# Splitting the attention's keys and queries in the dense stretch, with its sums on one engine

## The chip, the core and the metric

The kernel runs on one core of a Trainium2 chip. TensorE (PE) multiplies matrices into PSUM banks; VectorE (DVE), ScalarE (ACT) and GpSimd (POOL) do the elementwise work; SyncE (SP) issues most of the DMAs. Each engine works through its own queue of instructions in order, and semaphores tie the queues together: an instruction at the head of a queue that waits holds everything behind it. The metric is the device time of one execution in microseconds.

## What is computed

One layer of a hybrid encoder over 2048 tokens (a grid of 32 rows of 64) of width 1024. From the reference, cut:

```python
h = (_layernorm(x) * (1.0 + scale) + shift).astype(x.dtype)
proj = h @ w_in[l]
q_h, i_h, zf_fw, zf_bw, g_h, q_n, k_n, v_n, g_n = jnp.split(proj, split_pts, axis=-1)
y_hg = _hgrn2_branch(q_h, i_h, zf_fw, zf_bw, g_h, ...)
o_na = _neighbourhood_attention(na_heads(q_n), na_heads(k_n), na_heads(v_n), rpb[l])
y_na = o_na * jax.nn.silu(g_n)
y = jnp.concatenate([y_hg, y_na], axis=-1) @ w_out[l]
z = DEEPNORM_ALPHA * x + gate * y
x = _layernorm(z) * ln_g[l] + ln_b[l]
```

The neighbourhood attention has 16 heads of 64 columns; each query looks at a window of 8 rows by 16 columns. All is float32.

## The kernel before

TensorE takes its operands in a reduced form of float32. To keep the precision, every operand is split in a **high part** (a rounded copy, made by ACT) and a **low part** (the rest, a subtraction on DVE), and each product is three matmuls: high·high, high·low, low·high. So every weight, every tile of `h`, every key and query costs one ACT copy and one DVE subtraction before PE can use it.

The program goes through these stages, in one order on PE that is written out in the code:

- **Startup** (0 to about 91 us): LayerNorm and modulation of the first 1024 tokens in 16 blocks, two groups `g` of 512 tokens with 8 column tiles `k` each. Each block transposes x on PE (L236), ACT shifts and scales it (L241) and makes the high part (L243), DVE the low part (L1271), and PE then multiplies it with the first key, query and gate weights (L282). Between blocks, `values` (a generator over `vproj`, L295 on PE, evacuated on ACT at L303) computes the first part of the attention's values.
- **Dense stretch** (`dense_half`, to about 268 us): first `ahead()` gives PE a gate projection and more values, while `sum_piece` (L1405 on) makes the sums of h blocks that a seven-product scheme for 2x2 blocks needs: four additions of high and low on POOL (L1412), four sums on DVE (L1416), and a split of each (ACT L1419, DVE L1420). Then, for head pairs 1 to 7, class `Pair` multiplies the sums with combinations of the weights: `combine` (L1445 to 1450, POOL) and `prepare` (a split at L1459 and L1460) two products ahead, and `product` (L1475 on PE), whose results, keys `nk` and queries `nq` of 1024 tokens, go unsplit to DRAM.
- **First half of the attention** (`first_half`, to about 556 us): eight head pairs with four slots each. `natten_woven` computes scores (L1081, L1086, L1088), adds the bias and takes the maximum (DVE L1097), then exponent (ACT L1102), normalization (L1106, L1107), transposes (PE L1130, copied by DVE L1134 and ACT L1136) and the sum over the values (L1152). Between them `second_stream` gives PE dense work (L282, L295), and the second 1024 tokens of x are read (L199), measured (L206, L207), scaled and turned to h tiles `hs` in DRAM (`piece`: L241, L245, L250 and two stores, L1564 and L1565). What a slot prepares for the next pair stands in `first_next`: fetch keys and queries (`fetch_top`, L986), split them (`q` at L1000 to 1003, `k` at L1016 to 1018), load values (L1027) and bias tables (L757 to 759).
- The **HGRN recurrence** (to about 1740 us), the **second half of the attention** (to about 2270 us, prepared by `prep_next`), the **output projection**.

A key tile takes both heads of a pair, 64 partitions each. The score matmuls want `KA`, head 0's high part in both halves of the partitions, `KB`, the same of head 1, and `KL`, the low parts of both. `k` makes them by a copy on ACT, a DMA from half to half issued by POOL (L1017), and a subtraction on DVE. The first half has two sets of these tiles, so that one pair's can be made while the other's are read. In the second half there is one set, filled in pieces as the rows of the pair before come free.

On ACT, DVE, POOL and SP the order follows a scheduler that simulates the program, with high priorities where the code says so; in the startup SP, ACT and DVE are in code order as well. `pinned` keeps an instruction in code order. A tile takes one of its tag's buffers and waits until that is free: h tiles in flight to DRAM have three (`"s": 3`).

## Time and profile before

| | |
|---|---|
| three runs | 2586.09, 2587.28 (median), 2588.41 us |
| profiled execution | 2583.36 us |
| its span | 2581.4 us |
| busy: PE, DVE, ACT, POOL | 2529.1, 1883.8, 1502.3, 373.4 us |

The profile follows one execution; its span runs from the first instruction to the last. "Busy" is the time in which an engine executed something. For an engine that sets the pace, the idle time matters, and what ended it; for the others, idle time costs nothing by itself. A row `a <- b` names the instruction that waited and the work that released it. The granted clock is the share of its full speed that TensorE was allowed. Numbers behind L are lines of the kernel before.

### The profile page before, as it was taken

The page shows a single profiled execution, that of the slowest core. Times are in us where ns is not written, and L with a number is a line of the kernel's source. Part 1 is how long each engine was busy: PE and PEld are TensorE (multiplying, and loading weights), DVE is VectorE, ACT ScalarE, POOL GpSimd, SP SyncE. Part 2 cuts the span into 40 slices and gives each one's busy share as a digit, 9 for nine tenths or more (in the row PEclk, how much of TensorE's full clock was granted, in tenths as well). Part 3 has the DMA queues.
Part 4 walks back from the last instruction along what each step waited for, and adds up shares of the span by engine and source line. Part 5 has one row for each costly group of instructions (what it writes and reads, how often), then busy time and mean ns, then how long its engine had stood idle before and what let it go on. Part 6 is the DMA issues. An engine that isn't in the chain of part 4 may idle for free.

```text
span 2581.4 us, 46541 instructions
## 1 busy us (share of the span) xinstructions
PE 2529.1 (98%) x17040; PEld 2138.8 (83%) x17040; DVE 1883.8 (73%) x4567; ACT 1502.3 (58%) x2991; POOL 373.4 (14%) x485
## 2 busy tenths in 40 slices
PE   8899998999999999999999999999999999999998
PEld 7788877788888888888888888999888888888887
DVE  7745566668777778878778878746677778867776
ACT  5323355567666666767666666546677777752331
POOL 0422211200000000000000000011122222323542
PEclk9899999999999999999999999999999999999999
DMA  7445766612211115421222223345466667764452
GB/s 293 127 142 144 198 168 184 189 60 70 70 64 64 57 66 177 170 84 50 78 83 82 87 83 89 99 123 163 119 142 144 140 141 164 181 207 135 158 171 97
DMA packets 233604, 326.94 MB, mean 127 GB/s; under 512 B 42791, under 2 KB 115111, under 8 KB 232231
## 3 DMA queue, kind: packets, MB, share of 16 engines
q1 hardware_dynamic: 208383, 275.23, 35.1%
q0 software_dynamic: 24992, 48.73, 8.2%
q8 instruction: 134, 2.20, 0.4%
q14 instruction: 95, 0.78, 0.1%
HBM read 238.49 MB, written 77.08 MB: 122 GB/s over the span
## 4 chain that ended last, share of the span: by engine, by line
PE 80%; DVE 3%; DMA 2%; issue 1%; ACT 1%; POOL 0%; DVEq 0%; POOLq 0%; SPq 0%; ACTq 0%
PE pj L282 45%; PE pj L295 4%; PE ps L1839 3%; PE ps L1837 3%; PE ps L1838 3%; PE ps L1152 3%; PE ps L1130 3%; PE ps L488 2%; PE ps L480 2%; PE ps L1081 1%; PE ps L555 1%; PE ps L1086 1%; PE ps L584 1%; PE ps L586 1%; PE ps L527 1%
## 5 line engine op out<-in xcount | busy, mean ns | idle before, releaser
L282 PE MATMUL pj<-h,wh 128*128 128x512 f32 x3536 | 1130.1, 401 | 1.2 <-ACT vt L303 1.1
L282 PEld LDWEIGHTS pj<-h,wh 128*128 128x128 f32 x3536 | 640.0, 189 | 133.2 <-issue 10.1
L282 PE MATMUL pj<-h,wl 128*128 128x512 f32 x1768 | 695.0, 393 | 0.0
L282 PEld LDWEIGHTS pj<-h,wl 128*128 128x128 f32 x1768 | 333.0, 188 | 73.3
L295 PE MATMUL pj<-wh,h 128*128 128x256 f32 x1024 | 200.7, 289 | 10.8 <-ACT e L797 5.7
L1102 ACT ACTIVATE pbuf<-pbuf,mx 128x480 f32<-128x480 f32 (+5 forms) x256 | 152.4, 597 | 99.0 <-DVE mx L1097 98.4
L1097 DVE CUSTOM_DVE_ANT_1 pbuf<-ps,bias 128x480 f32<-128x480 f32 (+5 forms) x256 | 129.2, 539 | 86.7 <-PE ps L1086 61.1
L295 PEld LDWEIGHTS pj<-wh,h 128*128 128x128 f32 x1024 | 166.9, 195 | 14.8 <-ACT e L797 6.5
L273 DVE TENSOR_TENSOR wl<-wr,wh 128x512 fp32r<-128x512 f32 x192 | 131.4, 685 | 40.2 <-ACT wh L272 38.2
L272 ACT ACTIVATE wh<-wr 128x512 fp32r<-128x512 f32 x192 | 120.2, 626 | 68.5 <-PE pj L282 62.1
L295 PE MATMUL pj<-wl,h 128*128 128x256 f32 x512 | 146.6, 286 | 0.0
L1821 POOL TENSOR_TENSOR yl<-yr,yh 128x512 fp32r<-128x512 f32 (+1 forms) x80 | 108.6, 1367 | 148.6 <-ACT yh L1820 115.6
L1136 ACT ACTIVATE pt<-ps 120x384 f32<-120x384 f32 (+3 forms) x128 | 65.3, 510 | 95.3 <-PE ps L1130 94.8
L1130 PE MATMUL ps<-ident,pbuf 128*128 128x128 f32 (+2 forms) x832 | 114.7, 275 | 1.5 <-ACT s L241 0.6
L1130 PEld LDWEIGHTS ps<-ident,pbuf 128*128 128x128 f32 (+2 forms) x832 | 98.0, 138 | 19.9 <-DVE pbuf L1107 1.9
L474 DVE TENSOR_TENSOR de<-e,de 128x512 f32<-128x512 f32 x64 | 44.3, 691 | 87.8 <-ACT de L473 87.8
L1820 ACT ACTIVATE yh<-yr 128x512 fp32r<-128x512 f32 (+1 forms) x80 | 47.9, 607 | 102.0 <-PE ps L1838 42.2
L1107 DVE TENSOR_SCALAR pbuf<-pbuf,mx 128x480 f32<-128x480 f32 (+5 forms) x256 | 100.5, 414 | 3.0
L295 PEld LDWEIGHTS pj<-wl,h 128*128 128x128 f32 x512 | 100.0, 195 | 1.1
L1134 DVE COPY pt<-ps 120x384 f32<-120x384 f32 (+3 forms) x128 | 74.8, 584 | 34.2 <-PE ps L1130 33.4
L773 POOL MEMSET pbuf<- 128x248 f32 x8 | 2.1, 306 | 655.2 <-DVE pm L573 641.9
L455 DVE TENSOR_TENSOR_SCAN c<-c,g 128x128 f32<-128x128 f32 x256 | 88.6, 406 | 7.4 <-ACT c L445 7.4
(399 smaller groups left out, 5440.2 us busy)
## 6 DMA issues: line engine op xcount, KB each, us to landing
wr<-in_w_in SPq DMA_DIRECT2D x264, 256.0 KB
yr<-yq SPq DMA_DIRECT2D x78, 256.0 KB
bias<-tint POOLq DMA_DIRECT2D x24, 480.0 KB, 7.9
x<-in_x SPq DMA_DIRECT2D x32, 256.0 KB
ada<-in_ada_m SPq DMA_DIRECT2D x8, 1024.0 KB
wr<-in_w_v SPq DMA_DIRECT2D x32, 256.0 KB
nv<-vt SPq DMA_DIRECT2D x32, 256.0 KB
hs<-s SPq DMA_DIRECT2D x32, 256.0 KB
```

The costliest lines, as they stand in the source:

```text
L272: act.activation(hi, raw, AF.Copy)
L273: dve.tensor_tensor(lo, raw, hi, op=ALU.subtract)
L282: pe.matmul(pz, a, b, start=(k == 0 and n == 0), stop=(k == KT - 1 and n == 2))
L295: pe.matmul(pzs[tp][:, i * 256:(i + 1) * 256], a, b, start=(k == 0 and n == 0 and i == 0), stop=(k == KT - 1 and n == 2), skip_group_check ...
L455: dve.tensor_tensor_scan(c[:, sl], c[:, sl], L[:, sl], 0.0, op0=ALU.add, op1=ALU.subtract)
L1097: return dve.tensor_tensor_reduce(s[:, 0:nk].rearrange("p (r c) -> p r c", c=kw), sc[:, 0:nk].rearrange("p (r c) -> p r c", c=kw), bt[:, 0 ...
L1102: act.activation(s[:, 0:nk], s[:, 0:nk], AF.Exp, scale=-1.0, bias=mx[:, 0:1], accum_out=mx[:, 1:2])
L1107: dve.tensor_scalar(s[:, 0:nk], s[:, 0:nk], mx[:, 2:3], 1.0, op0=ALU.mult, op1=ALU.mult)
L1130: pe.transpose(ptp[0:cw, c * P:(c + 1) * P], s[:, c * cw:(c + 1) * cw], ident)
L1152: pe.matmul(self.po[R][hs_, j * P:(j + 1) * P], v[:, hh * 64:hh * 64 + 64], pts[hh][0:n * KW[j], c * P:(c + 1) * P], start=(c == 0), stop= ...
L1821: pool.tensor_tensor(lo[:, c], src[:, c], hi[:, c], op=ALU.subtract)
L1837: pe.matmul(bank, yh[:, kk], wh, start=start, stop=False, skip_group_check=True)
```

## The change

Four things are done at once.

**The sums.** `sum_piece` makes its four additions on DVE, and lets the four sums come before the four splits; `combine` runs on DVE too. POOL has no arithmetic left in the dense stretch. The second chunk of the value projection no longer stands between startup blocks: `startup` returns the generator, and `ahead()` runs it behind the last block. The four `sum_piece` calls come at steps 0, 3, 6, 9 of that longer stream (0, 4, 8, 10 of the shorter one before). While `feed.fast` is set, a weight's split has a high priority and is not pinned.

**The splits.** `product` splits keys (j = 2 and 5) and the queries of the first 512 tokens (j = 6) at once and stores high and low parts, `nkh` and `nqs`. Queries of the other half (j = 4) are stored unsplit, as before.

**The loads.** For pairs 1 to 7 the first half of the attention loads `KA`, `KB`, `KL` and both query tiles ready-made, seven DMAs on SP in slots 0 and 1 of the pair before, with no work on ACT, DVE or POOL. In the second half the pieces `k0` and `k1` of these pairs come the same way by five DMAs each, issued by POOL. Pair 0 stays as it was.

**The pieces of x.** Loads, statistics, rates and scaling of the second 1024 tokens are cut in smaller portions with a slot each (`at`), and the `hs` tiles move from a tag with three buffers to one with four (`"hb": "bk"`).

```diff
-            self.keep = p in (0, 7) if half else p > 0
+            self.keep = half and p in (0, 7)
...
+        def keys_in(self, o, at, dma=dma):
+            keys, n = keysets[self.p % len(keysets)], o.stop - o.start
+            for z, x in (("KA", slice(0, 64)), ("KB", slice(64, 128))):
+                for y in (slice(0, 64), slice(64, 128)):
+                    dma(keys[z][y, o].bitcast(F32), nkh_d[self.p][0, x, at:at + n])
+            dma(keys["KL"][:, o].bitcast(F32), nkh_d[self.p][1, :, at:at + n])
...
+            if self.half and i < 2 and self.p:
+                return self.keys_in(slice(a * GW, b * GW), (KBASE[1] + a) * GW, nc.gpsimd.dma_start)
...
-        return {0: [(st.fetch_top,), (st.v, 0)], 1: [(st.table, "top", 0), (st.v, 1), (st.k, 0)], 2: [(st.v, 2), (st.k, 1), (st.q, 0)],
-                3: [(st.table, "top", 1)]}
+        return {0: [(st.top_keys,), (st.v, 0)], 1: [(st.table, "top", 0), (st.top_queries,), (st.v, 1)], 2: [(st.v, 2)], 3: [(st.table, "top", 1)]}
...
-    NB0 = {"V": 6, "pbuf": 4, "pt": 4, "yv": 1, "bias": 3, "x": 8, "s": 3}
+    NB0 = {"V": 6, "pbuf": 4, "pt": 4, "yv": 1, "bias": 3, "x": 8, "s": 2}
...
-            pool.tensor_tensor(a, block_of(name, k, 0), block_of(name, k, 1), op=ALU.add)
+            dve.tensor_tensor(a, block_of(name, k, 0), block_of(name, k, 1), op=ALU.add)
...
+            if j in (2, 5):
+                hi, lo = tl("kh", F32R), tl("kh", F32R)
+                act.activation(hi, c, AF.Copy)
+                dve.tensor_tensor(lo, c, hi, op=ALU.subtract)
+                g = int(j == 5)
+                for i, z in enumerate((hi, lo)):
+                    dma(nkh_d[self.u][i, :, g * GRP:(g + 1) * GRP], z.bitcast(F32))
+            elif j == 4:
+                dma(nq_d[self.u][:, GRP:2 * GRP], c)
+            elif j == 6:
+                self.st.q(0, c)
+                for i, z in enumerate(self.st.Q.pop(0)):
+                    dma(nqs_d[self.u][i], z.bitcast(F32))
...
+            for _ in values:
+                feed.tick()
+                yield
             yield from gate_stream(preps[1], feed, (1,))
...
-            if i in (0, 4, 8, 10):
-                sum_piece((0, 4, 8, 10).index(i))
-            if i == 8:
+            if i in (0, 3, 6, 9):
+                sum_piece(i // 3)
+            if i == 14:
                 pairs[0].load(0)
...
-            a, b = short(F32R), short(F32R)
+            a, b = tl("hb", F32R), tl("hb", F32R)
...
-        for g, i in ((0, 3), (1, 16)):
-            slots[i].append((rows, g))
-            slots[i + 1].append((stats, g, 0))
-            slots[i + 2].append((stats, g, 2))
-            slots[i + 3].append((scale, g, 0))
-            slots[i + 6].append((scale, g, 1))
+        for g, at in ((0, (0, 1, 2, 3, 3, 4, 5, 6, 7, 8, 9, 11, 12, 10)), (1, (14, 15, 18, 18, 16, 17, 20, 21, 22, 22, 23, 25, 26, 24))):
```

What this does to the queues is shown at three places; lines there are those of each version, so L282 and L295 of before are L284 and L297 of the changed kernel.

PE at the end of the startup, before: the last matmuls of one block (`h_120` and `h_121` are the high and low part of an h tile, `q_421` and `q_422` of a weight), then the values (`pj`), of which twelve rows like these stand between each two blocks of the second group.

```order
L282 MATMUL ps_697<-h_120,q_421 128x512
L282 MATMUL ps_697<-h_121,q_421 128x512
L282 MATMUL ps_697<-h_120,q_422 128x512
L295 MATMUL pj_718<-wh_529,h_120 128x256
L295 MATMUL pj_718<-wl_530,h_120 128x256
L295 MATMUL pj_718<-wh_529,h_121 128x256
```

The same place of the changed kernel, and the end of the last block.

```order
L284 MATMUL ps_697<-h_120,q_421 128x512
L284 MATMUL ps_697<-h_121,q_421 128x512
L284 MATMUL ps_697<-h_120,q_422 128x512
L284 MATMUL ps_695<-h_122,vt_425 128x512
L284 MATMUL ps_695<-h_123,vt_425 128x512
L284 MATMUL ps_695<-h_122,gt_426 128x512
L284 MATMUL ps_696<-h_122,bk_417 128x512
L284 MATMUL ps_696<-h_123,bk_417 128x512
L284 MATMUL ps_696<-h_122,bk_418 128x512
L284 MATMUL ps_697<-h_122,q_421 128x512
L284 MATMUL ps_697<-h_123,q_421 128x512
L284 MATMUL ps_697<-h_122,q_422 128x512
```

The blocks follow each other directly, and all 96 of these value matmuls come behind the last.

DVE around the last low part of h, before: `h_119` to `h_123` are low parts, `wl` a weight's, `q_` the sums and `S_` the sums' low parts; the `sg` tiles come from POOL.

```order
L1271 TENSOR_TENSOR h_119<-sg_843,h_118 128x512
L1271 TENSOR_TENSOR h_121<-sg_873,h_120 128x512
L849 TENSOR_TENSOR wl_899<-wr_632,wh_898 128x512
L1271 TENSOR_TENSOR h_123<-sg_907,h_122 128x512
L1416 TENSOR_TENSOR q_986<-sg_978,sg_980 128x512
L1416 TENSOR_TENSOR q_992<-q_986,sg_982 128x512
L1420 TENSOR_TENSOR S_0_1_189_989<-q_986,S_0_0_188_988 128x512
L1416 TENSOR_TENSOR q_998<-sg_982,sg_978 128x512
```

The same place of the changed kernel; L1423 are the additions that were POOL's, L1286 is L1271 of before, L1427 and L1431 are L1416 and L1420.

```order
L1286 TENSOR_TENSOR h_119<-sg_781,h_118 128x512
L1286 TENSOR_TENSOR h_121<-sg_799,h_120 128x512
L1423 TENSOR_TENSOR sg_864<-h_108,h_109 128x512
L1423 TENSOR_TENSOR sg_866<-h_116,h_117 128x512
L1423 TENSOR_TENSOR sg_868<-h_92,h_93 128x512
L1427 TENSOR_TENSOR q_872<-sg_864,sg_866 128x512
L1286 TENSOR_TENSOR h_123<-sg_817,h_122 128x512
L1423 TENSOR_TENSOR sg_870<-h_100,h_101 128x512
L1427 TENSOR_TENSOR q_874<-q_872,sg_868 128x512
L1423 TENSOR_TENSOR sg_944<-h_110,h_111 128x512
L1431 TENSOR_TENSOR S_0_1_183_889<-q_872,S_0_0_182_888 128x512
```

Four operations of the sums now stand ahead of the last low part of h, and the weight's split has gone from between.

SP in the first half of the attention, before, while pair 2 is prepared: `bk` are unsplit queries and keys, `wr` weights of the dense work, `nv` the values' way to DRAM, `x` the second half of x.

```order
L199 DMA x_3049<-in_x 128x512
L838 DMA wr_2810<-in_w_in 128x512
L986 DMA bk_3104<-nq 128x512
L838 DMA wr_2890<-in_w_in 128x512
L838 DMA wr_2932<-in_w_v 128x512
L986 DMA bk_3106<-nk 128x256
L986 DMA bk_3473<-nk 128x512
L307 DMA nv<-vt_3004 128x2x256
```

The changed kernel, pair 2's keys and queries.

```order
L840 DMA wr_3015<-in_w_in 128x512
L992 DMA KA_549_2596<-nkh 64x768 x2
L992 DMA KB_550_2597<-nkh 64x768
L840 DMA wr_3057<-in_w_v 128x512
L992 DMA KB_550_2597<-nkh 64x768
L993 DMA KL_551_2598<-nkh 128x768
L1001 DMA q_3311<-nqs 128x512
L1001 DMA q_3312<-nqs 128x512
L309 DMA nv<-vt_3121 128x2x256
```

Seven loads replace three; the first write to a tile waits until PE has read what the pair two before left there.

More of the change, by code (lines that the diff above doesn't have):

```diff
@@ L1388, in startup @@
                 next(values)
-            else:
+            elif not g:
                 next(values, None)
-            if g:
-                feed.tick()
-        for _ in values:
-            pass
-        return rows, feed, first
+        return rows, feed, first, values
     AB = {"11": (0, 0), "12": (0, 4), "21": (1, 0), "22": (1, 4)}
@@ L1543, in first_half, with rows, stats, rates @@
         pipe, xs = [], {}
[L1545 to L1559 removed]
+        mvs, how, sts = {}, {}, {}
+        def rows(g, a, rs):
+            if g not in xs:
+                xs[g], mvs[g] = [[None, None] for _ in range(4)], x_mv()
+            for i in rs:
+                xs[g][i][a] = tl("x")
+                r0 = (2 + g) * GRP + i * P
+                dma(xs[g][i][a], x[r0:r0 + P, a * 512:(a + 1) * 512])
+        def stats(g, a, rs):
+            for i in rs:
+                if a == 0:
+                    sts[g, i] = cp.tile([P, 2, 6], F32, tag="bnst", name=nm("bnst"), bufs=4)
+                pinned(dve.bn_stats(sts[g, i][:, a, :], xs[g][i][a]))
+                if a:
+                    dve.bn_aggr(mvs[g][:, i, :], sts[g, i])
+        def rates(g):
+            how[g] = x_rates(mvs[g])
+        def scale(g, a, rs):
+            x_scale(xs[g], how[g], a, rows=rs, pin=pinned)
         def piece(g, k):
[L1562 removed]
+            a, b = tl("hb", F32R), tl("hb", F32R)
             h_piece(xs[g], k, a, b)
@@ L1647, in body @@
         with phase("st", SB_, SMS), tc.manual_schedule(engines={getattr(mybir.EngineType, e) for e in ("PE", "SP", "Activation", "DVE")}):
-            raws, feed, first = startup()
+            raws, feed, first, values = startup()
         with phase("sa", SA_, SMA):
@@ L1651, in body @@
             second = Chunks(second_srcs())
-            dense_half(preps, feed, first, second)
+            dense_half(preps, feed, first, values, second)
         with phase("n0", NB0, SM0):
```

81 lines of the change are left out of this document (40 added, 41 removed).

## The prediction

> **What bounds the kernel now.** I read the table of windows first, cut at the stages: first projections and sums (80 to 140 us), the seven pairs of dense products (140 to 280), the first half of the attention (280 to 560), the recurrence, the second half of the attention. Columns are stretch, length, busy us of PE, PEld, DVE, ACT and POOL, granted clock, DMA share, GB/s.
>
> ```profile
> 80.00:140.00 60.00, 48.82 (x306) 45.24 (x305) 44.03 (x43) 22.99 (x40) 30.68 (x19) 0.89 0.35 115
> 140.00:280.00 140.00, 140.00 (x622) 115.92 (x621) 78.30 (x128) 47.33 (x80) 38.56 (x39) 1.00 0.57 152
> 280.00:560.00 280.00, 261.53 (x1687) 216.65 (x1686) 175.55 (x514) 148.34 (x333) 50.48 (x96) 0.96 0.59 166
> 560.00:1740.00 1180.00, 1179.54 (x8952) 1004.73 (x8951) 910.59 (x2209) 769.99 (x1419) 7.09 (x21) 1.00 0.27 88
> 1740.00:2270.00 530.00, 528.87 (x3742) 448.00 (x3740) 400.71 (x1204) 372.28 (x855) 121.20 (x209) 1.00 0.63 151
> ```
>
> TensorE is the bound nearly everywhere: 140.00 of 140, 1179.54 of 1180, 528.87 of 530 us. The change removes no matmul, so where PE never idles nothing can be won. It idles 60 − 48.82 = 11.2 us in the first stretch and 280 − 261.53 = 18.5 us in the third; those two are what the change can reach. The list of PE's waits says for whom (us in total, times, longest); first 80 to 140, then 280 to 560:
>
> ```profile
> PE pj L295 <- ACT vt L303: 5.1, 1, 5.1
> PE pj L295 <- ACT e L797: 5.0, 1, 5.0
> PE pj L282 <- ACT vt L303: 1.1, 1, 1.1
> ...
> PE ps L1081 <- DVE mx L1097: 5.4, 2, 3.4
> PE ps L236 <- DVE pt L1134: 5.2, 1, 5.2
> PE ps L1081 <- issue: 3.3, 2, 2.0
> PE ps L1081 <- DMA KB<-KB: 1.8, 4, 1.1
> PE ps L1081 <- DVE pbuf L1107: 1.2, 1, 1.2
> PE ps L1130 <- ACT s L241: 0.6, 1, 0.6
> PE pj L295 <- ACT e L797: 0.4, 1, 0.4
> ```
>
> A gap costs more than itself, since the granted clock falls behind it. Three short windows around gaps:
>
> ```profile
> 98.00:108.00 10.00, 4.99 (x24) 4.78 (x24) 10.00 (x10) 3.71 (x7) 6.94 (x5) 0.66 0.23 65
> ...
> 334.00:346.00 12.00, 8.51 (x44) 6.43 (x43) 9.20 (x33) 6.00 (x16) 3.41 (x7) 0.75 0.54 160
> ...
> 312.00:320.00 8.00, 5.83 (x22) 4.52 (x22) 3.30 (x11) 1.50 (x6) 1.84 (x4) 0.79 0.98 237
> ```
>
> The clock's loss is 10 × 0.34 = 3.4 us, 12 × 0.25 = 3.0 and 8 × 0.21 = 1.7. Over the stages it is 60 × 0.11 = 6.6 and 280 × 0.04 = 11.2 us. About 2.6 of the 6.6 falls into time in which PE idled anyway. So the ceiling is 11.2 + 4.0 = 15 us in the first stretch and 18.5 + 11.2 = 30 in the third, 45 together.
>
> **Where a short gap counts.** The 2.00 us gap at 314 stands in the window of 0.79: gaps of 2 us already slow PE. The Trainium skill, "TensorE: Matmul & The Clock Gate", says under "Why this matters for your kernels" that the clock drops for idle gaps over about 3 us; by that the 2 us gaps here cost themselves only, and some 5 us of the third stretch's clock loss would not come back. The row differs, and I go by the row.
>
> **Sums on DVE alone.** Groups of 80 to 126 us (busy, mean ns | idle before), DVE, then POOL, then ACT:
>
> ```profile
> L1420 DVE TENSOR_TENSOR S<-q,S 128x512 fp32r<-128x512 f32 x16 | 18.1, 1155 | 0.0
> L1416 DVE TENSOR_TENSOR q<-sg,sg 128x512 f32<-128x512 f32 x8 | 7.6, 955 | 0.0
> L1416 DVE TENSOR_TENSOR q<-q,sg 128x512 f32<-128x512 f32 x4 | 5.8, 1460 | 0.2
> ...
> L1416 DVE TENSOR_TENSOR q<-sg,q 128x512 f32<-128x512 f32 x4 | 4.9, 1222 | 0.0
> L1271 DVE TENSOR_TENSOR h<-sg,h 128x512 fp32r<-128x512 f32 x2 | 1.4, 692 | 3.8 <-ACT h L243 3.8
> ...
> L1412 POOL TENSOR_TENSOR sg<-h,h 128x512 f32<-128x512 f32 x14 | 23.1, 1671 | 10.9 <-DVE q L1416 5.5 <-DVE h L1271 5.3
> ...
> L1419 ACT ACTIVATE S<-q 128x512 fp32r<-128x512 f32 x16 | 10.0, 629 | 22.4 <-DVE q L1416 22.4
> ```
>
> Thirty-two additions on DVE take 36.4 us, 1.14 each; the same form away from POOL's takes 0.69 (L1271). ACT waits 22.4 us for them, and its evacuations e and vt stand behind those waits in its queue; that is how PE's two 5 us gaps come about. The change moves POOL's 16 additions over: 48 × 0.69 = 33.1 us on DVE in place of 36.4, with POOL silent. So the sums alone get only 3 us shorter. The larger part is order: the weight splits are put ahead of sums (feed.fast), and the second chunk of the value projection moves from between the last startup blocks to just behind them:
>
> ```profile
> 85.58 0.28 PE L295 MATMUL pj<-wh,h 128*128 128x256 f32 x1
> ...
> 87.02 0.63 PE L282 MATMUL ps<-h,vt 128*128 128x512 f32 x2
> ```
>
> Twelve matmuls take 87.02 − 85.58 = 1.44 us in each of eight blocks, 11.5 us of PE work that no longer delays the last h tile and covers the sums instead. Its price: a block has 1.44 us less cover for its own chain, transpose, ACT twice, DVE once. I take 2.3 us lost there, since near the end four sums stand ahead of h's last low part (4 × 0.69 = 2.8 us less what is idle). Behind it I count about 1.0 at the gate stream, 0.7 at its evacuation, 2.2 where two splits of sums stand ahead of vt on ACT (3 × 0.63): 6.2 us lost in place of 15. **Gain 9**, bounds 5 (the 3 us of DVE and part of the order) and 13.
>
> **Splits in the dense products.** Each of seven pairs gains on DVE two low parts, four combines from POOL and two half-width low parts: 8 × 0.69 = 5.5 us; ACT gets four copies by 0.63, 2.5 us; SP three more stores. In the stretch DVE goes from 78.3 to 78.3 + 38.6 = 117 of 140 us, ACT from 47 to 65. Combines and splits of before:
>
> ```profile
> L1450 POOL TENSOR_TENSOR gt<-wr,gt 128x512 f32<-128x512 f32 x3 | 4.8, 1588 | 19.0 <-DVE wl L1460 13.4 <-DMA wr<-in_w_in 5.7
> ...
> L1460 DVE TENSOR_TENSOR wl<-gt,wh 128x512 fp32r<-128x512 f32 x19 | 14.6, 767 | 8.0 <-ACT wh L1459 8.0
> ```
>
> A split of 767 ns against 692 shows that POOL's 28 combines disturbed DVE little here; silence returns about 3 us, which leaves 114 of 140 and PE the bound. Zero. If the cover is gone (eight operations of a pair in a row hold the next weights), a pair loses up to 1.5 us, seven 10.
>
> **First half of the attention.** Per pair 1 to 7 the change drops ACT's copies and DVE's low parts of keys and queries, and POOL's copies from half to half; five key loads and two query loads on SP take their place, a slot or more ahead. Groups of 280 to 560, then what DVE waited for there:
>
> ```profile
> L206 DVE BATCH_NORM_STATS2 bnst<-x 128x6 f32<-128x512 f32 x16 | 10.2, 671 | 0.1
> ...
> L1018 DVE TENSOR_TENSOR KL<-bk,KB 64x512 fp32r<-64x512 f32 (+1 forms) x14 | 7.8, 556 | 0.4
> L1018 DVE TENSOR_TENSOR KL<-bk,KA 64x512 fp32r<-64x512 f32 (+1 forms) x14 | 7.6, 545 | 2.8 <-ACT KA L1016 2.8
> ...
> L1003 DVE TENSOR_TENSOR q<-bk,q 64x512 fp32r<-64x512 f32 x7 | 4.8, 688 | 0.2
> L1002 DVE TENSOR_TENSOR q<-bk,q 64x512 fp32r<-64x512 f32 x7 | 4.8, 685 | 0.4 <-ACT q L1000 0.2
> ...
> DVE s L245 <- DMA hs<-s: 12.5, 2, 8.2
> ```
>
> DVE loses 7.8 + 7.6 + 4.8 + 4.8 = 25 of 175.6 us. By cause:
> - copies KA/KB: "issue" 2.0 (the other 1.3 is pair 0's, which keeps them) and KB 1.8, with 1.7 of clock: 5.5, all gone.
> - mx, 5.4 and about 5.1 of clock: eight of L206, the key splits and the scale chain stand ahead of L1097. The change spreads statistics over four slots and takes the splits out. Three quarters: 7.9.
> - pt, 5.2 and 3.4: L245 held DVE 8.2 us until a store of hs released one of three buffers. Now four, with x's loads spread. Four fifths: 7.
> - the rest, 2.2 and 1.7: half, 2.
>
> That is 22.4. The key loads are new on SP, in order, waiting for PE's scores of two pairs before, with weight loads queued behind. By the rows the cost lies between nothing (a pair has 280 / 8 = 35 us, and they go out a pair ahead) and one 2 us gap with its 1.7 per pair, 7 × 3.7 = 26. I take 2.4, nearer to nothing, as there are several slots. **Gain 20**, bounds 0 and 28.
>
> **Second half.** Keys k0 and k1 of pairs 1 to 7 come by ten loads on POOL in place of four copies on POOL, two fetches on SP and eight instructions on ACT and DVE. POOL's copies, a bias load and its use:
>
> ```profile
> L1017 POOL DMA_DIRECT2D KA<-KA x37 | 19.9, 538 | 72.6 <-ACT KA L1016 59.7 <-PE ps L1086 12.1
> ...
> 1894.66 0.63 POOL L755 DMA_DIRECT2D bias<-tint  x1
> ...
> 1902.24 0.66 DVE L1097 CUSTOM_DVE_ANT_1 pbuf<-ps,bias 128x480 f32<-128x480 f32 x1 [0.39 <-PE ps L1086]
> ...
> DMA to landing us min/median/max: 4.0/6.9/15.1
> ```
>
> Six more issues by 0.54 are 3.2 us per pair, in two places; behind them wait the bias loads, one of which has 1902.24 − 1894.66 = 7.6 us for a landing of 6.9. PE is full here, so nothing can be won. Zero, bounds a gain of 1 (PE's idle) and a loss of 43 (below).
>
> **Sum.** The profiled execution took 2583.36 us: 2581.4 of span and 2.0 around it. 2583.4 − 9 − 20 = 2554.4. The median of the runs shown, 2587.28, is 3.9 above that execution; kept, this gives **2558.3**.
>
> **Rivals.**
> - *Bias late in the second half* (the slower side). If 3.2 us of later issue and 2 of slower landing (a quarter of the way from 6.9 to the longest, 15.1) make a bias 5.2 late, 4.5 past the slack of 0.7, that is 6.2 with 1.7 of clock, in seven pairs 43: 2558 + 43 = 2601. From about 35 us, 5 per pair, the kernel is measurably slower. For it: the short slack above, DMA share 0.63. Against: POOL idled 72.6 us before those copies, and they waited in the same queue. Chance 0.07.
> - *Key loads late in the first half*: SP's queue holds them, the gaps stay under another name, and only the start's 9 and a part return: 2587.3 − 13 = 2574. For it: DMA share 0.98 around 314. Against: a pair's lead. Chance 0.15.
> - *DVE bounds the sums*: 48 additions with splits between them still reach the first product late; the start gives 1: 2566. For it: 33 against 36 us. Chance 0.15.
> - *The change doesn't do what it says*: the spread pieces of x meet new waits and everything cancels: 2587. Chance 0.06.
> - *Clock by the long gaps only*: the 2 us gaps' clock loss stays, 5 us: 2563. The row of 0.79 speaks against. Chance 0.03.
>
> My forecast (gain 20 to 42) has 0.54. Range 2545 (42 of the ceiling of 45) to 2581: it leaves out half the fourth rival, the first, and tails, about 0.17. 0.2% is 5.2 us, about what a measurement of this kernel can tell from no change. Faster: 0.54 + 0.15 + 0.15 + 0.03 = 0.87; same 0.06; slower 0.07.
>
> **What would show it.** Windows of 80 to 140 with POOL near nothing, DVE's sums at about 0.69 and clock over 0.95; the waits on e and vt below 2.5 us. In 280 to 560 PE over 274 busy, no wait for KB, pt or hs. In 1740 to 2270 PE still above 528. Wrong if PE waits for key or query loads, for the ps banks in the products, or for the bias.

## The result and the profile after

| | before | changed |
|---|---|---|
| four runs, median | 2586.69 us (2582.83 to 2588.41) | 2563.34 us (2561.01 to 2564.43) |
| ratio, 95% interval | | 0.9911 [0.9893, 0.9928] |
| profiled execution | 2583.36 us | 2563.62 us |
| its span | 2581.4 us | 2561.8 us |

The change saves 0.9%. It was forecast at 2558.3 us, in a range of 2545 to 2581. In two of the experiments below, one execution of four was far longer than the others (8833.1 and 4168.6 us), and the medians given there leave it out. Where the 19.5 us of span went is seen best from PE's own marks, read from the timelines of both kernels (us of each stage; a stage ends with the first matmul of the next, and the second half of the attention is counted from its first score with low parts):

| stage on PE | before | changed | difference | forecast |
|---|---|---|---|---|
| to the first dense product | 134.66 | 123.45 | −11.2 | −9 |
| the 49 dense products, first to last | 133.08 | 133.08 | 0 | 0 |
| last product to the first score ("the join") | 18.58 | 24.71 | +6.1 | none made |
| first score to the recurrence | 260.25 | 242.69 | −17.6 | −20 |
| recurrence | 1201.40 | 1201.21 | −0.2 | 0 |
| second half of the attention | 556.62 | 560.14 | +3.5 | 0 |
| output projection | 276.80 | 276.56 | −0.2 | 0 |

The windows of the changed kernel, with the same columns as before (stretch, length, busy of PE, PEld, DVE, ACT, POOL, granted clock, DMA share, GB/s):

```profile
80.00:140.00 60.00, 59.13 (x393) 54.27 (x392) 43.86 (x71) 25.06 (x44) 0.00 (x0) 1.00 0.39 125
140.00:280.00 140.00, 136.17 (x602) 112.75 (x601) 99.90 (x169) 60.42 (x102) 7.81 (x17) 0.98 0.62 187
280.00:560.00 280.00, 269.29 (x1858) 224.96 (x1858) 172.56 (x528) 144.56 (x328) 33.23 (x66) 0.99 0.71 187
...
1740.00:2270.00 530.00, 525.80 (x3656) 441.46 (x3655) 388.02 (x1171) 356.68 (x821) 141.71 (x247) 1.00 0.64 157
```

The first row is full: PE 59.13 of 60 us at a clock of 1.00, from 48.82 at 0.89. The third has 269.29 in place of 261.53. The second and the last have each lost some 3 to 4 us of PE. PE's list of waits (us in total, times, longest) says where, first 60 to 130 us, then 250 to 560, then 1700 to 2270. Line numbers are now those of the changed kernel (and in an experiment's rows, those of that run's kernel, which can lie a few lines further on):

```profile
PE ps L284 <- DVE h L1286: 0.7, 2, 0.5
PE pj L297 <- ACT vt L305: 0.5, 1, 0.5
PE pj L297 <- ACT e L799: 0.3, 1, 0.3
...
PE ps L238 <- ACT pt L1152: 7.2, 1, 7.2
PE ps L1097 <- DVE mx L1113: 1.5, 1, 1.5
PE pj L297 <- ACT wh L851: 1.4, 1, 1.4
...
PE ps L1097 <- DMA KA<-KA: 2.1, 1, 2.1
PE ps L1097 <- DMA yr<-yq: 1.1, 2, 0.5
```

The two 5 us waits of the start (e, vt) are 0.3 and 0.5. In the first half of the attention the maximum (mx) went from 5.4 to 1.5 and no wait for KA or KB is left, but the wait of a transpose for a bank (L238, in the kernel before L236) has grown from 5.2 to 7.2. It is now the largest single wait of the kernel between the startup and the end.

### The profile page after: what moved, and what is told of

It is laid out like the page before. It is cut to its first block, busy times and chain, and to the rows that moved or that the text cites. A ratio compares the mean times of both kernels' runs of the same rounds, so it can differ in the third digit from the quotient of the medians.

```text
span 2561.8 us, 46445 instructions
## 1 busy us (share of the span) xinstructions
PE 2519.8 (98%) x17040; PEld 2130.8 (83%) x17040; DVE 1869.9 (73%) x4569; ACT 1483.0 (58%) x2949; POOL 316.1 (12%) x455
## 4 chain that ended last, share of the span: by engine, by line
PE 88%; DVE 2%; DMA 2%; issue 1%; ACT 1%; POOL 0%; SPq 0%; DVEq 0%; POOLq 0%; ACTq 0%
PE pj L284 46%; PE pj L297 6%; PE ps L1486 5%; PE ps L1874 3%; PE ps L1873 3%; PE ps L1872 3%; PE ps L1168 3%; PE ps L1146 3%; PE ps L490 2%; PE ps L482 2%; PE ps L1097 2%; PE ps L557 1%; PE ps L1102 1%; PE ps L586 1%; PE ps L588 1%
## 5 line engine op out<-in xcount | busy, mean ns | idle before, releaser
L284 PE MATMUL pj<-h,wh 128*128 128x512 f32 x3536 | 1127.2, 400 | 0.0
L284 PEld LDWEIGHTS pj<-h,wh 128*128 128x128 f32 x3536 | 638.5, 188 | 131.5 <-issue 10.1
L284 PE MATMUL pj<-h,wl 128*128 128x512 f32 x1768 | 693.6, 392 | 0.9 <-DVE wl L854 0.9
L284 PEld LDWEIGHTS pj<-h,wl 128*128 128x128 f32 x1768 | 331.9, 188 | 74.2 <-DVE wl L854 1.3
L1118 ACT ACTIVATE pbuf<-pbuf,mx 128x480 f32<-128x480 f32 (+5 forms) x256 | 152.4, 597 | 125.1 <-DVE mx L1113 124.5
L1113 DVE CUSTOM_DVE_ANT_1 pbuf<-ps,bias 128x480 f32<-128x480 f32 (+5 forms) x256 | 129.2, 540 | 113.3 <-PE ps L1102 73.9
L297 PE MATMUL pj<-wh,h 128*128 128x256 f32 x1024 | 198.4, 288 | 4.9 <-ACT vt L305 1.8
L297 PEld LDWEIGHTS pj<-wh,h 128*128 128x128 f32 x1024 | 165.1, 194 | 9.2 <-ACT vt L305 2.6
L297 PE MATMUL pj<-wl,h 128*128 128x256 f32 x512 | 146.0, 285 | 0.4 <-DVE wl L854 0.4
L1152 ACT ACTIVATE pt<-ps 120x384 f32<-120x384 f32 (+3 forms) x128 | 65.1, 509 | 94.1 <-PE ps L1146 93.5
L297 PEld LDWEIGHTS pj<-wl,h 128*128 128x128 f32 x512 | 99.2, 194 | 1.4 <-DVE wl L854 0.6
```

Source lines behind the costliest of these rows:

```text
L284: pe.matmul(pz, a, b, start=(k == 0 and n == 0), stop=(k == KT - 1 and n == 2))
L297: pe.matmul(pzs[tp][:, i * 256:(i + 1) * 256], a, b, start=(k == 0 and n == 0 and i == 0), stop=(k == KT - 1 and n == 2), skip_group_check ...
L1113: return dve.tensor_tensor_reduce(s[:, 0:nk].rearrange("p (r c) -> p r c", c=kw), sc[:, 0:nk].rearrange("p (r c) -> p r c", c=kw), bt[:, 0 ...
L1118: act.activation(s[:, 0:nk], s[:, 0:nk], AF.Exp, scale=-1.0, bias=mx[:, 0:1], accum_out=mx[:, 1:2])
```

## Experiments: the start

Each edit is against the changed kernel ("−" is the changed kernel). Times are medians; ratios are against the kernel before on the same chip. Stage times come from one profiled execution of each kernel, and kernels whose edit doesn't touch a stage still differ there: the first dense product came at 122.4 to 123.8 us in eight kernels, the first half of the attention took 242.0 to 245.1 us in five, and the second half 557.3 to 562.0 us in twelve. Differences below these widths aren't read.

**The additions back on POOL**, everything else as changed.

```diff
-            dve.tensor_tensor(a, block_of(name, k, 0), block_of(name, k, 1), op=ALU.add)
+            pool.tensor_tensor(a, block_of(name, k, 0), block_of(name, k, 1), op=ALU.add)
```

> The changed kernel with the sixteen additions of high and low parts back on POOL (the combines of the weights stay on DVE). Two theories of the start's gain, read at the first product's matmul (134.7 us from the span's start before, 123.5 changed). Order theory: the gain comes from the value matmuls behind the last block and from splits that go ahead of sums; POOL's additions slow DVE's to about 1.1 us again, but most of the cover stays: first product at 126 to 129, the whole 3 to 5 us slower than the changed kernel. Port theory: the gain comes from POOL being silent; then nearly all is lost: first product at 132 or later, the whole 8 to 12 us slower.

Measured 2574.02 us, ratio 0.9949 [0.9931, 0.9966]; the first product at 134.96 us. The whole 11 us of the start are gone, though the new order is in place. The groups of this run, 78 to 126 us on DVE, then POOL's to 128 us (count, busy, mean ns, idle before):

```profile
L1431 DVE TENSOR_TENSOR S<-q,S 128x512 fp32r<-128x512 f32 x16 | 14.8, 951 | 0.0
L854 DVE TENSOR_TENSOR wl<-wr,wh 128x512 fp32r<-128x512 f32 x6 | 7.3, 1220 | 0.0
...
L1423 POOL TENSOR_TENSOR sg<-h,h 128x512 f32<-128x512 f32 x13 | 21.8, 1701 | 8.6 <-DVE q L1427 7.4 <-DVE h L1286 1.2
```

and the changed kernel's, 78 to 122 us:

```profile
L1431 DVE TENSOR_TENSOR S<-q,S 128x512 fp32r<-128x512 f32 x16 | 10.9, 689 | 2.1 <-ACT S L1430 2.1
L1423 DVE TENSOR_TENSOR sg<-h,h 128x512 f32<-128x512 f32 x14 | 9.4, 688 | 0.0
...
L854 DVE TENSOR_TENSOR wl<-wr,wh 128x512 fp32r<-128x512 f32 x6 | 4.1, 690 | 0.0
```

Weight splits, too, take 1.22 us each in place of 0.69 while POOL adds, six of them 3.2 us more. DVE's idle time before its rows is 0.0 with POOL adding: it didn't stand waiting for POOL's results, it was slow. PE again waits for vt (4.15 us at 96) and e (5.72 us at 111), as in the kernel before.

**The order of before, the sums on DVE.** The value matmuls stand between the startup blocks again, `feed.fast` is never set, the sums come at steps 0, 4, 8, 10.

```diff
-            elif not g:
+            else:
                 next(values, None)
+            if g:
+                feed.tick()
+        for _ in values:
+            pass
...
-            feed.fast = True
             preps[1].raws["g"][0] = first
-            for _ in values:
-                feed.tick()
-                yield
...
-            if i in (0, 3, 6, 9):
-                sum_piece(i // 3)
-            if i == 14:
+            if i in (0, 4, 8, 10):
+                sum_piece((0, 4, 8, 10).index(i))
+            if i == 8:
```

> The changed kernel with the order of the start undone: value matmuls again between the startup blocks, sums again at steps 0, 4, 8, 10, splits of weights pinned and without priority; the sums stay on DVE alone. Order theory: first product at 129 to 133 us, the whole 6 to 10 us slower than the changed kernel. Port theory: with POOL silent the sums are fast wherever they stand: first product at 124 to 126, the whole within 3 us of the changed kernel.

Measured 2561.18 us, 0.9904 [0.9887, 0.992]; the first product at 120.29 us, 3.2 us earlier than in the changed kernel. So the new order costs about 3 us at this mark, where the prediction had most of the 9 us from it; the whole time is the same within its interval. The window of 60 to 80 us of the changed kernel, then of this one:

```profile
60.00:80.00 20.00, 19.24 (x95) 14.96 (x94) 11.19 (x22) 11.97 (x18) 0.00 (x0) 1.00 0.56 148
```

```profile
60.00:80.00 20.00, 20.00 (x129) 18.04 (x127) 8.04 (x17) 9.41 (x15) 0.00 (x0) 1.00 0.57 143
```

PE loses 0.76 us there, since part of a block's chain is no longer covered. Behind it the changed kernel's waits on vt and e, 0.5 and 0.3, are gone here as well: from 15 to 258 us this run has no gap of PE of over 0.2 us. Together that is 1.6 of the 3.2 us; the rest wasn't resolved. The four sums ahead of the four splits and the combines on DVE stay as changed in this run.

Both experiments can be read from ACT's wait for the sums, behind which e and vt stand in its queue. It was 22.4 us in the kernel before. Here it is from 60 to 126 us with the additions back on POOL, in the changed kernel, and with the order of before:

```profile
ACT S L1430 <- DVE q L1427: 19.7, 11, 3.5
```

```profile
ACT S L1430 <- DVE q L1427: 7.1, 6, 3.6
```

```profile
ACT S L1434 <- DVE q L1431: 6.3, 2, 6.0
```

It follows the engine of the additions and not the order.

**The additions on DVE, and the same sixteen again on POOL** into tiles that nobody reads, so that both engines are busy and nothing depends on POOL.

```diff
             dve.tensor_tensor(a, block_of(name, k, 0), block_of(name, k, 1), op=ALU.add)
+            pool.tensor_tensor(tl("s"), block_of(name, k, 0), block_of(name, k, 1), op=ALU.add)
```

> The changed kernel, with the additions on DVE as they are and in the same order, and the same sixteen additions once more on POOL, into scratch tiles that nobody reads. Port theory, POOL's and DVE's additions slow each other: DVE's additions of 80 to 122 us go from 0.69 to over 1.0 us in the mean, first product from 123.5 to 130 or later, although nothing waits for POOL. Rival, the start was slow before because sums waited for POOL's results: additions stay at 0.69 and the first product at 123 to 125.

One execution: 2573.55 us, the first product at 133.32 us: work that nobody waits for costs 9.9 us of the start. DVE's timeline (start, duration, instruction; x3 is three in a row), then POOL's group:

```profile
75.06 1.77 DVE L1286 TENSOR_TENSOR h<-sg,h 128x512 fp32r<-128x512 f32 x1 [1.18 <-ACT h L245]
76.75 5.13 DVE L1423 TENSOR_TENSOR sg<-h,h 128x512 f32<-128x512 f32 x3
...
97.72 0.68 DVE L1423 TENSOR_TENSOR sg<-h,h 128x512 f32<-128x512 f32 x1
```

```profile
L1424 POOL TENSOR_TENSOR s<-h,h 128x512 f32<-128x512 f32 x10 | 16.9, 1725 | 0.0
```

The same instruction on DVE takes 5.13 / 3 = 1.71 us at 76.75 and 0.68 us at 97.72, when POOL is done: a DVE operation lasts as long as one of POOL's. The low part of h (L1286), on which PE waits in the startup, goes from 0.69 to 1.77 in the same way. POOL slows down too: its additions take 1.29 us where DVE has nothing running (at 59.94, and at 74.07 in the kernel before) and 1.7 us beside DVE.

The 9.9 us come by another path than the 11.2 that the change saved, so their likeness is chance. In this run POOL adds without a pause from 70.8 to 94.8 us, earlier than in the kernel before; PE waits 6.1 us for the last low part of h, which stands behind four slowed operations of the sums, and 2.8 us for vt. In the kernel before h's low parts were not slowed (0.692 us, in the prediction's groups). What the run does show is that a busy POOL is enough to slow DVE, with no dependence between them. The Trainium skill, "GPSIMD Engine Reference", "8. Key points", says that GpSimd shares its SBUF interfaces with VectorE and contends with DVE instructions that have two SBUF inputs. These rows agree, and give the price that the section leaves out: 1.0 us per operation of 128x512.

## Experiments: the first half of the attention

**The pieces of x as before.** Loads, statistics and scaling of x stand in the slots of the kernel before, with three buffers for h tiles; keys and queries still come ready-made.

```diff
-    NB0 = {"V": 6, "pbuf": 4, "pt": 4, "yv": 1, "bias": 3, "x": 8, "s": 2}
+    NB0 = {"V": 6, "pbuf": 4, "pt": 4, "yv": 1, "bias": 3, "x": 8, "s": 3}
...
-            a, b = tl("hb", F32R), tl("hb", F32R)
+            a, b = short(F32R), short(F32R)
...
-        for g, at in ((0, (0, 1, 2, 3, 3, 4, 5, 6, 7, 8, 9, 11, 12, 10)), (1, (14, 15, 18, 18, 16, 17, 20, 21, 22, 22, 23, 25, 26, 24))):
...
+        for g, i in ((0, 3), (1, 16)):
+            slots[i].append((rows, g))
+            slots[i + 1].append((stats, g, 0))
+            slots[i + 2].append((stats, g, 2))
+            slots[i + 3].append((scale, g, 0))
+            slots[i + 6].append((scale, g, 1))
```

> The changed kernel with the pieces of x as before (eight loads at once, statistics in two portions, h tiles in flight in three buffers); keys and queries are still loaded ready-made. From the first score to the recurrence's first transpose it is 260.3 us before and 242.7 changed. Theory 1: the spreading and the fourth buffer took away the wait for the stores of h tiles and half the crowd ahead of the maxima: 8 to 12 us are lost, with a wait of 5 us or more for a store of an h tile. Theory 2: the gain there is that of the ready-made keys and queries alone, and the spreading only moved the wait for the stores (7.2 us of PE at 415 us in the changed kernel): within 3 us of 242.7.

Measured 2575.96 us, 0.9962 [0.9949, 0.9975]. The stage takes 255.03 us: 12.3 above the changed kernel, 5.2 below the one before. So the ready-made keys and queries without the new pieces of x are worth 5.2 us, and the pieces of x on top of them 12.3; the pieces of x alone were not run. PE's wait for the maximum is 0.3 us here, and its wait for a bank (L238) 12.1. DVE's waits, 280 to 540 us, of this kernel:

```profile
DVE s L247 <- DMA hs<-s: 29.1, 7, 11.4
...
DVE s L252 <- DMA hs<-s: 15.7, 10, 4.3
```

With three buffers DVE stood 29.1 + 15.7 = 44.8 us for stores of h tiles. The changed kernel's list, 280 to 524 us, has less of the same, 21.2 us, not none:

```profile
DVE bk L247 <- DMA hs<-bk: 16.4, 5, 8.7
...
DVE bk L252 <- DMA hs<-bk: 4.8, 5, 3.2
```

In the kernel before, with three buffers and the same pieces, the two lines came to 12.5 + 1.5 = 14.0 us. So the rest of the change tripled this wait, and the fourth buffer with the spread pieces took only part of that back. What tripled it isn't shown; the key loads' place on SP alone isn't it, as the wait is still 18.4 us when they are issued by POOL (a run below).

**What that wait does** is followed through the changed kernel's timeline. PE, then ACT, then DVE (in brackets the idle time before the row and its releaser):

```profile
407.72 0.40 PE L284 MATMUL pj<-h,wl 128*128 128x512 f32 x1
415.36 1.12 PE L238 MATMUL ps<-ident,x 128*128 128x128 f32 x4 [7.24 <-ACT pt L1152]
```

```profile
413.20 0.59 ACT L1118 ACTIVATE pbuf<-pbuf,mx 128x352 f32<-128x352 f32 x1 [11.63 <-DVE mx L1113]
...
414.84 0.47 ACT L1152 ACTIVATE pt<-ps 96x384 f32<-96x384 f32 x1
```

```profile
387.75 0.43 DVE L247 CAST bk<-s 128x512 fp32r<-128x512 f32 x1
...
410.24 0.43 DVE L247 CAST bk<-s 128x512 fp32r<-128x512 f32 x1 [8.73 <-DMA hs<-bk]
...
412.65 0.51 DVE L1113 CUSTOM_DVE_ANT_1 pbuf<-ps,bias 128x352 f32<-128x352 f32 x1
```

From the bottom up: at 410 DVE has waited 8.73 us at L247 for a buffer; the maximum L1113 stands behind it on DVE; ACT's exponent L1118 waits 11.63 us for the maximum; the copy L1152, behind the exponent on ACT, frees a bank only at 415; PE's transposes L238 wait 7.24 us for that bank. Why the store was late is in SP's rows. The tile that held the buffer, two before in the ring of four, was made at 387.75, and SP stores it (L1598) at 401.55. First SP's rows, then one of SP's waits from 385 to 412 us:

```profile
390.15 0.37 SPq L1598 DMA_DIRECT2D hs<-bk  x1
...
392.49 1.67 SPq L1579 DMA_DIRECT2D x<-in_x  x2
394.25 0.39 SPq L840 DMA_DIRECT2D wr<-in_w_in  x1
394.74 0.86 SPq L1579 DMA_DIRECT2D x<-in_x  x2
398.69 1.44 SPq L992 DMA_DIRECT2D KA<-nkh  x2
400.32 0.44 SPq L840 DMA_DIRECT2D wr<-in_w_in  x1
401.55 0.33 SPq L1598 DMA_DIRECT2D hs<-bk  x1
```

```profile
SPq L992 <- DMA hs<-bk: 3.0, 1, 3.0
```

Between the two stores stand four loads of x, two of keys and two of weights (and, left out above, two of values and the store of a low part). SP waits too: 3.0 us ahead of L992, until the store issued at 390.61, eight issues ahead, had landed. The store at 401.55 in turn went out when the load of x issued at 392.49, again eight ahead, had landed 9.0 us after its issue. So in these rows an issue waits for the DMA eight places ahead of it, and slow landings hold the queue; the DMA share was 0.95 to 1.02 in the windows from 395 to 410. Four experiments ask which part of that matters.

**No key loads for one pair.** Pair 5's five key loads, which stand in this place, are left out; its scores are computed with the keys of pair 3.

```diff
-            self.keys_in(slice(0, 12 * GW), 0)
+            if self.p != 5:
+                self.keys_in(slice(0, 12 * GW), 0)
```

> The changed kernel with the loads of pair 5's keys in the first half left out (1.15 MB of about 6 that go between 385 and 412 us); pair 5 is computed with the keys of pair 3. Theory 1 (DMA engines full): the store of the h tile lands in 6 us or less, the gap at 415 us falls below 3 us, first score to recurrence 232 to 237 us. Theory 2 (three buffers' worth of pieces are in flight for another reason, as SP issues the stores late behind other loads): the gap stays over 5 us, 240 to 245.

One execution: 2564.17 us, the stage 241.37 us, and PE's gap is still there, 7.71 us at 413. DVE's row:

```profile
407.99 0.43 DVE L247 CAST bk<-s 128x512 fp32r<-128x512 f32 x1 [10.41 <-DMA hs<-bk]
```

This pair's key loads aren't what makes the store late; SP has enough else ahead of it.

**Key loads a slot later.**

```diff
-        return {0: [(st.top_keys,), (st.v, 0)], 1: [(st.table, "top", 0), (st.top_queries,), (st.v, 1)], 2: [(st.v, 2)], 3: [(st.table, "top", 1)]}
+        return {0: [(st.v, 0)], 1: [(st.table, "top", 0), (st.top_keys,), (st.v, 1)], 2: [(st.top_queries,), (st.v, 2)], 3: [(st.table, "top", 1)]}
```

> The changed kernel with the ready-made keys and queries of the first half loaded one slot later (slots 1 and 2 of the pair before, not 0 and 1), so that those of pair 5 no longer follow right on four loads of x. In the changed kernel DVE waits 8.7 us at 401 us for the store of an h tile, the share of the DMA engines is 0.85 to 1.04 from 390 to 415 us, and PE idles 7.2 us and is slow for 6.8. Theory 1, the DMA engines are full there because loads of x, keys and stores fall together: with a slot between them the gap at 415 us falls below 3 us, first score to recurrence 242.7 goes to 233 to 237. Theory 2, the loads are only moved into the next crowd (the other four loads of x come two slots later): 240 to 246, the wait for a store stays over 5 us.

Measured 2568.0 us, 0.9938 [0.9919, 0.9958]; the stage 246.36 us. The gap at 413 is 8.35 us, and PE now waits for queries (`q<-nqs`, 1.8 us at 488). Nothing is won, and queries that were not waited for now are.

**The stores of h on POOL's queue.**

```diff
-            dma(hs[k][:, 0, g * GRP:(g + 1) * GRP], a.bitcast(F32))
-            dma(hs[k][:, 1, g * GRP:(g + 1) * GRP], b.bitcast(F32))
+            nc.gpsimd.dma_start(hs[k][:, 0, g * GRP:(g + 1) * GRP], a.bitcast(F32))
+            nc.gpsimd.dma_start(hs[k][:, 1, g * GRP:(g + 1) * GRP], b.bitcast(F32))
```

> The changed kernel with the sixteen pairs of stores of h tiles in the first half issued by POOL and not by SP. In the changed kernel, and also without pair 5's key loads, an h tile made at 387 us is stored only at 401: SP issues in order, each DMA waits until the one eight places ahead has landed, and at 395 to 405 us these take some 8 us each. Theory 1, SP's order holds the stores: on a queue of their own they go out within 2 us of the tile, DVE's wait for a store (8.7 us) falls below 2, the gap of 7.2 us at 415 us goes, first score to recurrence from 242.7 to 231 to 235, the whole 7 to 11 us faster. Theory 2, the DMA engines are full and the stores take as long on any queue, or POOL's queue holds them behind bias loads that wait: 239 to 244.

Measured 2556.41 us, 0.9885 [0.9861, 0.9909]; the stage takes 235.42 us, 7.3 less than in the changed kernel. PE's longest wait of 250 to 560 us, then DVE's wait for data (280 to 524), then the issues of these stores (count, KB, median us to landing):

```profile
PE ps L238 <- ACT pt L1152: 3.9, 1, 3.9
```

```profile
DVE bnst L1585 <- DMA x<-in_x: 9.6, 3, 5.0
```

```profile
hs<-bk POOLq DMA_DIRECT2D x32, 256.0 KB, 5.6
```

DVE's list has no line for `hs` any more. The bytes are the same, only the queue has changed: the wait was SP's order. PE's wait of 3.9 us that is left, at 407, now comes right behind DVE's of 5.0 us for a load of x. (The whole time's interval still overlaps that of the changed kernel, 0.9893 to 0.9928; it is the stage that is clear of its width.) The Trainium skill, "DMA: Bandwidth & Descriptors", "Issuing engines are not separate DMA queues", says that DMAs from several engines end on the same 16 DMA engines, and that several issuers save only the time of issuing, usually small. Here that isn't all: one store's issue takes 0.35 us in SP's rows, and what was saved is the 13 us for which a ready store stood behind other issues and their waits.

**The key loads of this half on POOL's queue** in place of SP's, with the stores on SP again.

```diff
-            self.keys_in(slice(0, 12 * GW), 0)
+            self.keys_in(slice(0, 12 * GW), 0, nc.gpsimd.dma_start)
```

> The changed kernel with the ready-made keys of the first half issued by POOL (five per pair) and not by SP; the stores of h tiles stay on SP. If SP's queue is the limit (theory 1), thirty-five fewer DMAs in it shorten the stores' delay: the gap at 415 us falls, though x's loads and the values still stand ahead of the stores, 236 to 241 us from first score to recurrence. If the engines are the limit (theory 2), 241 to 245, and POOL's bias loads come later.

Measured 2570.33 us, 0.9935 [0.9917, 0.9953]; the stage takes 249.27 us, longer than either theory said. PE's waits, 250 to 560 us:

```profile
PE pj L297 <- ACT vt L305: 8.1, 1, 8.1
PE ps L238 <- ACT pt L1152: 4.5, 1, 4.5
```

A new gap of 8.1 us stands at 385, the old one at 422 is 4.5. The new one is the same chain as before: DVE stands 10.47 us at L247, until 381.59, for the store of an h tile, and ACT's exponent waits 11.18 us behind it. So not every relief of SP's queue helps; here the stores were as late as before. Why they were, with the key loads gone from SP, stays open.

## Experiments: the join, the second half, and all together

**The join.** In the changed kernel ACT's row in front of the first scores, and SP's row that made it wait:

```profile
269.02 0.63 ACT L1052 ACTIVATE sg<-e 128x512 f32<-128x512 f32 x1 [2.91 <-DMA nqs<-sg]
```

```profile
259.83 1.04 SPq L1513 DMA_DIRECT2D nqs<-sg  x2
```

A gate (L1052) needs a buffer of tag "sg", which the last pair's query parts hold until their stores have landed; those went out at 259.83. The weight splits stand behind the gate on ACT, and PE has three gaps from 270 to 274 us, 1.4 + 0.4 + 1.0, and 6.83 us at half clock behind them. The experiment puts the query parts in another tag:

```diff
-    ... "kh": "vt", "Q": "sg", "x": "sg"}
+    ... "kh": "vt", "Q": "vt", "x": "sg"}
```

> The changed kernel with the query tiles that the dense stretch stores taken from another group of buffers (that of the key tiles and the values) and no longer from that of the gates. In the changed kernel ACT waits 2.9 us at 269 us for the last pair's query stores, since a gate needs their buffer, and a weight's split stands behind it; PE then idles 2.9 us in three gaps and runs at half clock for 6.8 us. Theory 1, the buffer is the cause: first score at about 275 us in place of 281.25, the whole 5 to 6 us faster. Theory 2, ACT and DVE are simply crowded there with the last pair's splits and the first pair's pieces: first score within 1.5 us of 281.25, the whole the same.

Measured 2561.09 us, 0.9904 [0.9889, 0.9919]. The first score comes 281.25 − 276.79 = 4.5 us earlier, though now it waits 2.0 us for pair 0's key copy, which those gaps had covered:

```profile
PE pj L297 <- ACT vt L305: 5.0, 1, 5.0
PE ps L1097 <- DMA KA<-KA: 2.0, 1, 2.0
```

The join takes 20.77 us, so the buffer was the cause of 3.9 of its 6.1. But the first half gives it back, 247.57 us against 242.69, with a new gap of 5.0 at 377: the work that arrives earlier meets the same stores (DVE waits 7.6 us at L247, until 373.18, for one).

**The second half's pieces k0 and k1 by SP** in place of POOL.

```diff
-                return self.keys_in(slice(a * GW, b * GW), (KBASE[1] + a) * GW, nc.gpsimd.dma_start)
+                return self.keys_in(slice(a * GW, b * GW), (KBASE[1] + a) * GW)
```

> The changed kernel with the keys k0 and k1 of the second half issued by SP and not by POOL. From the second half's first score to the output projection's first matmul of its last stretch it is 556.6 us before and 560.1 changed, with 3.2 us of new waits of PE for KA, KB at 2184 to 2209 us. Theory 1, five issues on POOL in place of two hold up POOL's later copies: with SP these waits go, 556 to 557.5. Theory 2, the later copies are late because of DMA traffic or of their own place in the queue: 559 to 561. If SP's queue holds something PE needs, it is more.

Measured 2563.93 us, 0.9915 [0.9896, 0.9935]; the second half 559.56 us. The two half-microsecond waits at 2184 are gone, the one for the last pair's KA copy stays, 2.3 us. That is within the 557.3 to 562.0 us of the kernels that issue from POOL, so nothing here speaks for POOL's extra issues as the source of the 3.5 us.

**Together**: the order of before in the startup and the stores on POOL (the edits of the second and of the stores' experiment), without and with the other tag.

> The same without the edit of the query tiles: the order of the start undone, and the stores of h tiles on POOL. If the two add up: 2563.3 less 3 and 7, 2552 to 2555. If the edit of the query tiles is worth nothing where the stores no longer wait, this equals the run with three edits; if it is worth its 4.5 us there, this is 3 to 5 us slower than that.

> Three edits of the changed kernel together: the order of the start undone (first product 3.2 us earlier by itself), the stored query tiles in another group of buffers (first score 4.5 us earlier by itself), the stores of h tiles on POOL (first half of the attention 7.3 us shorter by itself). If they add up: 15 us below the changed kernel's 2563.3, 2547 to 2551. If earlier work only meets later loads of x and keys, which came with the query tiles' edit alone (its 4.5 us were given back at 376 us), the start's 3 and the stores' 7 remain: 2551 to 2556.

| | median us | ratio | first product | first half |
|---|---|---|---|---|
| stores on POOL alone | 2556.41 | 0.9885 [0.9861, 0.9909] | 122.45 | 235.42 |
| and the order of before | 2555.77 | 0.9891 [0.9872, 0.9911] | 120.44 | 238.11 |
| and the other tag | 2555.07 | 0.9882 [0.9867, 0.9897] | 119.82 | 242.14 |

The three are equal within their intervals, 30 us below the kernel before and 7 to 8 below the changed one, though their intervals still overlap or touch that one's. Each step makes the first half start earlier, and it takes about as much longer: it ends at 515.7, 517.1 and 515.7 us. DVE's waits for x, 280 to 524 us, with order and stores changed, then with the tag too:

```profile
DVE bnst L1585 <- DMA x<-in_x: 13.3, 3, 10.9
```

```profile
DVE bnst L1585 <- DMA x<-in_x: 10.4, 3, 8.5
```

The longest wait for loads of x goes from 5.0 (stores alone) to 10.9 and 8.5, and PE's longest gap of the stage (5.4 us until 434, 7.5 until 406) ends 1.4 and 4.7 us behind it. I read it as the next limit: these loads stand in SP's queue. No kernel was run that moves them, so this is argued, not shown.

## Why the prediction was right, and where it was not

The sum was right to 5 us, and part of that was luck. Its terms were read from profiled executions, and there it gave 2554.4 us where 2563.62 was measured: a gain of 29 forecast, 19.8 measured. It then added 3.9 us, since the median of before lay that far above its profiled execution; the changed kernel's median lies 0.3 us below its own, so this took 4 us of the error back by chance. Of the terms, those of the start and of the first half came out near with part of their mechanism wrong, the join had none, and the second half's was too small.

- **Sums on DVE alone: 9 forecast, 11.2 measured; the mechanism was wrong.** The step that failed is "So the sums alone get only 3 us shorter. The larger part is order". With the additions back on POOL the order gave −0.3 us (134.96 against 134.66); with the order undone the rest of the edit gave 14.4 (134.66 − 120.29), about the whole ceiling of 15; in the new order the additions alone are worth 11.5 (134.96 − 123.45). The comparison of 36.4 us for 32 operations with 33.1 for 48 looked at DVE's total, and PE doesn't wait for that: it waits for ACT, which waits for single sums, 22.4 us before and 6.3 to 7.1 with the additions on DVE. How much of that is the sums at 1.14 us, and how much the weight splits at 1.2 us between them, wasn't separated. The rival "DVE bounds the sums" fell with it.
- **The order's price: 6.2 us forecast, 2.3 of it in the blocks; 3.2 measured** against the order of before. PE's waits left in this stretch are only 0.7 us in the blocks and 0.8 behind. The price was there, smaller, and the saving of 15 that it was to be taken from came from the other part of the edit.
- **Dense products: 0 and 0.** 133.08 us in every run, with DVE and ACT carrying the splits.
- **The join: +6.1, no term for it.** The prediction costed the splits where they are made, and not the buffers that they hold until stored. It is the step "SP three more stores" that lacked one question: who needs those buffers next. With the other tag 3.9 of the 6.1 us were gone.
- **First half: 20 forecast, 17.6 measured.** Copies KA/KB, 5.5, "all gone": right, no such wait is left. (The 5.2 us of the run with the old pieces of x is not this term: there the maximum's gaps were gone too, and the bank's had grown.) The maximum, 7.9: gaps of 5.4 became one of 1.5, without a stretch of lower clock, some 9 us; right in size. But with the statistics of x in two portions as before PE waited only 0.3 us for it, so the spread statistics weren't needed for this. The step that failed is "pt, 5.2 and 3.4 … Four fifths": that gap is 7.2 us with 6.83 us at half clock, larger than before. A fourth buffer and spread loads shortened the total wait for stores (44.8 to 21.2 us with the rest equal; 14.0 before the change) and left one of 8.7, as a store still stands behind eleven other issues. So this term was a loss of 2 and not a gain of 7. The gain came from the other gaps: 5.5, 9.0, 2.4 for the rest, less 2.0, and no cost of key loads, 14.9 in all; the other 2.7 of the 17.6 us weren't located. With the stores on POOL's queue the stage falls to 235.42, 24.8 below the one before, so the ceiling was there.
- **Key loads on SP, 2.4.** PE waited for none in the first half. The rival "SP's queue holds them, the gaps stay under another name" had the right queue and the wrong goods: stores were held, and taking a pair's key loads out left the gap.
- **Second half: 0 forecast, +3.5 measured**, inside the bounds. PE's gaps of the stage add up to it: 0.53 + 0.54 + 2.12 + 0.35. PE waited for no bias, so the slower rival fell. Its slack of 0.7 us had also been misread: the bias load issued at 1894.66 landed 13.7 us later, after the use at 1902.24, so the two rows don't belong together. Why pair 7's copy of KA lands 2 us later than before is open; it isn't POOL's number of issues. POOL issued that copy at 2206.07, after 3.25 us of waiting for ACT, though ACT's part of KA was done at 2202.58; in the kernel before it went out 0.4 us behind ACT's part.
- **The clock.** The rival by which only long gaps slow PE was to be told apart by gaps near 2 us, and these go both ways. Its 2563 us is the time measured, but by other terms: that is chance. The copy of KA makes PE wait 2.12 us in the changed kernel and 2.29 with k0 and k1 on SP. The windows of 2206 to 2216 us, first the changed kernel's:

```profile
2206.00:2216.00 10.00, 7.53 (x51) 5.83 (x51) 6.12 (x19) 5.75 (x13) 3.80 (x7) 1.00 0.73 199
```

```profile
2206.00:2216.00 10.00, 7.71 (x35) 6.22 (x33) 5.50 (x16) 5.06 (x11) 3.75 (x7) 0.83 0.70 205
```

The first keeps its clock at 1.00, the second drops to 0.83. A gap of 2 us may or may not cost clock, and to count it always was too much. What decides it isn't shown.

## What to carry to other kernels

Moving a two-operand operation from GpSimd to VectorE can shorten VectorE's own work, since in these runs the additions and subtractions there ran at GpSimd's pace meanwhile: look at the mean duration of one form with and without the other engine busy, and count every operation in the stretch. When a wait is for a buffer that a store must release, read the issuing queue's rows between the making of the tile and its store before adding buffers; moving the store to a queue that isn't full of loads was worth 7.3 us here. Gains at stages that follow each other need not add up: here the later stage ended at about the same time however early it began. And when a forecast is carried from one execution to a median, say what that step adds; here it hid 4 us of error.

## What was not expected of the hardware

- A subtraction or addition of 128x512 on DVE took 0.68 us alone and 1.71 to 1.77 beside POOL's additions of 1.73, which take 1.29 alone: both slow down, and they go in step.
- With the DMA share near 1, a store of 256 KB took 8.7 us from SP's issue at 401.55 to the release of its buffer at 410.24, on top of 13 us in the queue.
- A PE gap of 2.12 us left the granted clock at 1.00, one of 2.29 in the same place took it to one half for 3.41 us.
